# Gate products of the long sequence: half of them by pairs with seven half products, and moved ahead of the units

## The chip, the core and the metric

The kernel runs on one NeuronCore of a Trainium2 chip. The metric is device time of one launch in microseconds (us); the kernel before takes 2138.08 us in the median of three runs (2135.49 to 2138.51).

The core has five instruction queues. TensorE (PE) multiplies matrices out of the on-chip memory SBUF into accumulator banks (PSUM). VectorE (DVE), ScalarE (ACT) and GpSimd (POOL) do the elementwise work. SyncE (SP) issues most of the DMAs. Each queue runs in order, and semaphores tie the queues together.

## The reference, cut to what matters

One layer runs over a short sequence (`x_prompt`, 512 tokens) and a long one (`x_sample`, 1024 tokens), model width 1024:

```
u = x * (1 + scale) + shift                        # T x 1024
proj = u @ w_in                                    # nine segments, for the units A (HGRN2) and R (retention)
y_a, y_r = unit A(proj), unit R(proj)              # T x 1024 each
g_a, g_r = split(sigmoid(u @ w_mg + b_mg))         # w_mg is 1024 x 2048: the gates
s = (g_a * (y_a @ w_pa) + g_r * (y_r @ w_pb)) @ w_out
out = layer_norm(ALPHA * x + (1 + gate) * s) * ln_g + ln_b
```

The change concerns `u @ w_mg` of the long sequence.

## The kernel before, in words

Every large product has float32 accuracy: each operand is split into a high and a low part (type F32R), and three of the four part products are added, low activation times high weight, high times low, high times high. So one output piece of 128 columns by 512 tokens, with 1024 rows to sum over in k = 0 to 7, is 24 matmuls of 512 columns in one PSUM bank (`gemm_f`, L305). There are three such banks (`gbank`), used in turn; a bank is free again when ACT or DVE has read it.

The class `Stream` (L26) holds the weights in the order of use. A raw piece of 512 KB is loaded by SP into one of two buffers. `tick()` has ACT copy it to the high part (L94), `flush()` has DVE (in one stretch POOL) subtract to get the low part (L103). Four split pieces can stand ready.

The sequence g = 0 is the short one, g = 1 the long one, as two blocks b of 512 tokens. Each goes through units (8 A and 4 R for g = 1), then `gates(g)` (L814), then for each block `pblock` (products with `w_pa` and `w_pb`) and `oblock` (product with `w_out`, then layer norm). The order is written out by hand: `interleave` emits the steps of a large product (the filler) and between them stages of elementwise work, spread by weight, and the ticks of the weights. Within an engine, work runs in the order in which it was emitted.

`gates(1)` stands behind the last unit: two blocks of 16 pieces, each piece loaded and split for each block. After 512 columns ACT takes the sigmoid (L826) and issues the store to DRAM (`gd`, L827). In the last block the loads of `pblock`'s first operand `y` begin at the fifth piece (`load_y`, L843).

The layer norm of the last `oblock` of g = 0 ends in four `finish` stages (L911 to L930). In each, DVE makes mean and variance (L914), POOL makes the inverse root (L915, L916), DVE and ACT scale two halves (L919, L925, L928), POOL adds to one half (L929), and SP stores both (L930). They are handed over in `more` and are interleaved with `pre(us[0])`, the 144 matmuls that open the units of g = 1.

Of the kernel before, what the change touches and what calls it, by code (L numbers as in the profile page):

```python
# [17 lines left out]
ALPHA = 2.0 ** 0.25  # L18
LEVELS = (1, 2, 4, 8, 16, 32, 64)
# [6 lines left out]
class Stream:  # L26
    """The weights in order of use: raw pieces are loaded, split into two F32R parts, used, released."""

    def __init__(self, nc, raw_pool, w_pool, ring, raw_bufs, load):
        self.nc, self.raw_pool, self.w_pool = nc, raw_pool, w_pool  # L30
        self.ring, self.raw_bufs, self.load = ring, raw_bufs, load
        self.todo = []
        self.n_load = self.n_split = self.n_got = 0
        self.used = 0
        self.raws = {}
        self.tiles = {}
        self.parts = []
        self.lo = nc.vector
        self.rest = None

# [15 lines left out]
    def open(self, j):  # L56
        """the slots of a piece, if they are free"""
        kind, ps = self.todo[j]
        need = 2 if kind == "t" else 1
        if self.used + need > self.ring:  # L60
            return False
        self.used += need
        if kind == "t":
            h = self.w_pool.tile([128, NK, 256], F32R, name="wh", tag="w", bufs=self.ring)
            l = self.w_pool.tile([128, NK, 256], F32R, name="wl", tag="w", bufs=self.ring)
            self.tiles[j] = (h, l)
            self.parts = [(h[:, :, 128 * i:128 * i + 128], l[:, :, 128 * i:128 * i + 128]) for i in range(2)]
        else:
            shape = [128, 2, 768] if kind == "k" else [128, 2, NK, 128]
            w = self.w_pool.tile(shape, F32R, name="w", tag="w", bufs=self.ring)  # L70
            self.tiles[j] = (w[:, 0], w[:, 1])
            self.parts = [self.tiles[j]]
        return True

    def tick(self):
        """split the next raw piece, if there is room; its low part follows with flush()"""
        self.flush()
        self.pump_loads()
        j = self.n_split
# [9 lines left out]
        i = len(ps) - len(self.parts)  # L89
        hi, lo = self.parts.pop(0)  # L90
        raw = self.raws[j, i]
        if kind == "k":
            raw = raw.rearrange("p k n -> p (k n)")[:, 0:768]
        self.nc.scalar.activation(out=hi, in_=raw, func=AF.Copy)  # L94
        self.rest = (hi, lo, raw, j, i)
        return True

    def flush(self):
# [5 lines left out]
        del self.raws[j, i]  # L104
# [58 lines left out]
def layer(ctx, tc, x_p, x_s, c_p, c_s, w_ada, b_ada, w_in, hgrn_lb, a_norm_w, ret_decay, w_pa, w_pb, w_mg, b_mg,  # L163
# [5 lines left out]
    at = ctx.enter_context(tc.tile_pool(name="at", bufs=2))  # L169
    wp = ctx.enter_context(tc.tile_pool(name="wp", bufs=4))  # L170
    rp = ctx.enter_context(tc.tile_pool(name="rp", bufs=2))
    up = ctx.enter_context(tc.tile_pool(name="up", bufs=4))
    dp = ctx.enter_context(tc.tile_pool(name="scr", bufs=1, space=bass.MemoryType.DRAM))
# [4 lines left out]
    BUFS = {"X": 4, "T1": 2, "T2": 2, "T4": 2, "T8": 2, "T16": 2, "T32": 2, "T64": 2, "T128": 2, "KM": 2, "q": 2,  # L178
            "D": 2, "A": 2, "V": 3, "G": 3, "sg": 2, "Kt": 2, "S": 2, "y": 2, "yT": 2}

    def sb(tag, shape, dt=F32, name=None):
        return at.tile(shape, dt, name=name or tag, tag=tag, bufs=BUFS[tag])

# [30 lines left out]
    gd = [dp.tile([16, 128, NT[g]], F32, name=f"gd{g}") for g in range(2)]  # L214
    xs, outs = (x_p, x_s), (out_p, out_s)

# [32 lines left out]

    def order_pre(u):  # L250
        if u.kind == "A":
            for ls in u.wl:
                h = u.lanes[ls[0]][0]
                for seg in range(3):
                    ws.add("f", (w_in, 1024 * seg + 128 * h))
# [23 lines left out]
    for g in range(2):  # L279
# [4 lines left out]
        else:  # L284
            order_pre(us[0])
# [4 lines left out]
        for b in range(NT[g] // 512):  # L290
            for n in range(16):
# [13 lines left out]
    def gemm_f(ps, w, a):  # L305
        """ps[n, t] += sum_k w[k, n] a[k, t]; a: (hi, lo) as lists of [128, 512] over k"""
# [9 lines left out]
    def gemm_t(ps, w, a, t0, k0=0, k1=NK):  # L316
        """ps[t, n] += sum_k a[k, t] w[k, n]"""
# [49 lines left out]
    def pre_A(u):  # L367
        g = u.g
        prep_A(u)
        for ls in u.wl:  # L370
            for seg in range(3):
# [5 lines left out]
                ws.done(j)  # L377

# [27 lines left out]
    def update(u, l, h):  # L406
        """decays of blocks of h become those of blocks of 2h"""
# [406 lines left out]
    def gates(g):  # L814
        for b in range(NT[g] // 512):
            for n in range(16):
                j, w = ws.get()
                if b == NT[g] // 512 - 1:
                    if n == 4:
                        more_y = load_y(g, 0, 0)  # L820
                    if n >= 4 and more_y:
                        more_y.pop(0)()
                ps = gbank([128, 512])
                yield from gemm_f(ps, w, u_f(g, b))
                t = sb("sg", [128, 512])
                S.activation(out=t, in_=ps, func=AF.Sigmoid, bias=vec[:, 48 + n:49 + n])  # L826
                S.dma_start(gd[g][n, :, 512 * b:512 * b + 512], t)  # L827
# [78 lines left out]
    def oblock(g, b, st, last):  # L906
# [49 lines left out]
        # the last rows of s come last  # L956
# [62 lines left out]
    def u_parts():  # L1019
        """the next part of each product of u_stage that still lacks one"""  # L1020
# [6 lines left out]
    def ada_mm(ps, w):  # L1027
        """silu(c) times columns of w_ada: four sums over k, rows 32 j and 32 j + 1 of ps"""
# [4 lines left out]
    def ada_out(ps, row, jobs):  # L1033
        """the sum of the four, with the columns on the partitions, plus a bias and a constant"""
# [6 lines left out]
    def startup():  # L1041
# [47 lines left out]
        # silu(c) = c / (1 + exp(-c))  # L1089
# [12 lines left out]
        def bounds():  # L1102
# [3 lines left out]
            # softmax over the one layer, its cumulative sum less its first row  # L1106
# [11 lines left out]
        def log_sigmoids():  # L1118
            # lg = log_sigmoid(r) = min(r, 0) - log1p(e), e = exp(-|r|); log1p(e) = 2 atanh(z), z = e / (2 + e)
# [118 lines left out]
    PRE = {"A": 31.1, "R": 20.9}  # L1238
    MID = {"A": 20.9, "R": 41.9}

    def run(gen):
        for _ in gen:
            pass

    with tc.manual_schedule():
        startup()
        more = []
        for g in range(2):
            us = groups[g]
            if g:  # L1250
                interleave(pre(us[0]), 12.0, more, marks, ws)
            for i, u in enumerate(us):
                st = stages_A(u) if u.kind == "A" else stages_R(u)
                if i + 1 < len(us):
                    nx = us[i + 1]
                    interleave(chain(mid(u), pre(nx)), MID[u.kind] + PRE[nx.kind], st, marks, ws, LEAD_IN)
                else:
                    interleave(chain(mid(u), gates(g)), MID[u.kind] + 60.0, st, marks, ws)
            more = []
            nb = NT[g] // 512  # L1260
            for b in range(nb):
# [13 lines left out]
                more = st["finish"]  # L1275

# [51 lines left out]
```

## Time and profile before

| quantity | value |
|---|---|
| median of three runs | 2138.08 us (2135.49 to 2138.51) |
| profiled execution, span from first to last instruction | 2135.2 us |
| PE busy | 2108.5 us, 99% |
| DVE, ACT, POOL busy | 1122.3 us, 746.7 us, 437.7 us |
| share of the last chain that is PE | 95% |
| median of the runs less the span of the profile | 2.9 us |

The page gives no separate time for the profiled execution beyond its span; the lowest of the three runs lies 0.3 us above that span, the median 2.9 us.

How to read it: PE is busy for nearly the whole span, so a matmul that goes saves its own step, and a new wait of PE costs its own length. The elementwise engines are busy half the time or less, but what counts is whether they finish before PE asks for their result.

### The profile page before, as it was taken

Reading aid. Unit: us, or ns where it says so; the run is one execution under the profiler, and the core shown is the slowest. Engines: PE = TensorE matmul, PEld = TensorE weight load, DVE = VectorE, ACT = ScalarE, POOL = GpSimd, SP = SyncE. Lnnn points to the kernel's source line nnn. Section 1 sums busy time; section 2 is a strip of 40 time slices with the busy share of each in tenths; the row PEclk is TensorE's granted clock in tenths of the full one; section 3 lists DMA queues with packets and bytes.
Section 4 is the critical chain, followed back from the end, with each engine's and each line's share of the span. In section 5 each row is a group of like instructions: output and inputs, shape, how many; then the busy total and the mean of one; then the engine's idle time right before and its main releaser. Section 6 shows DMA issues by size and latency. Waiting matters only on the chain.

```text
span 2135.2 us, 45792 instructions
## 1 busy us (share of the span) xinstructions
PE 2108.5 (99%) x19331; PEld 1892.8 (89%) x19331; DVE 1122.3 (53%) x2242; ACT 746.7 (35%) x1570; POOL 437.7 (20%) x668
## 2 busy tenths in 40 slices
PE   7999999999999999999999999999999999999997
PEld 5898899998888988899889889999999888889887
DVE  4856764644334965554565457353543442245657
ACT  3644553223322534444444435212121233322221
POOL 3322233321000332121121214332322100000101
PEclk9999999999999999999999999999999999999999
DMA  9322323246776421111111211212212256577752
GB/s 285 111 84 85 92 85 106 70 129 187 226 243 201 140 80 61 41 50 61 41 61 41 70 31 61 65 41 65 85 40 85 84 163 211 185 234 225 242 184 80
DMA packets 340205, 247.29 MB, mean 116 GB/s; under 512 B 9564, under 2 KB 303680, under 8 KB 338976
## 3 DMA queue, kind: packets, MB, share of 16 engines
q1 hardware_dynamic: 332112, 229.75, 34.9%
q10 hardware_dynamic: 6944, 12.59, 1.5%
q8 instruction: 152, 2.49, 0.5%
q0 software_dynamic: 944, 2.02, 0.3%
q14 instruction: 53, 0.43, 0.1%
HBM read 199.23 MB, written 45.10 MB: 114 GB/s over the span
## 4 chain that ended last, share of the span: by engine, by line
PE 95%; DMA 1%; DVE 1%; POOL 1%; issue 1%; ACT 1%; SPq 0%; POOLq 0%; DVEq 0%; ACTq 0%
PE g L310 41%; PE g L321 38%; PE l L542 2%; PE l L430 2%; PE t L505 2%; PE l L459 1%; PE l L742 1%; PE l L740 1%; PE t L677 1%; PE g L1171 1%; PE t L489 1%; PE l L1171 1%; PE t L707 1%; PE l L725 1%; PE t L1031 1%
## 5 line engine op out<-in xcount | busy, mean ns | idle before, releaser
L321 PE MATMUL g<-wh,u 128*128 128x256 f32 x3840 | 736.2, 287 | 0.0
L310 PE MATMUL g<-u,w 128*128 128x512 f32 x2736 | 671.7, 397 | 0.0
L321 PEld LDWEIGHTS g<-wh,u 128*128 128x128 f32 x3840 | 609.5, 191 | 8.9 <-issue 4.0
L310 PEld LDWEIGHTS g<-u,w 128*128 128x128 f32 x2736 | 499.7, 188 | 100.7 <-issue 1.2
L321 PE MATMUL g<-wl,u 128*128 128x256 f32 x1920 | 542.6, 283 | 0.0
L321 PEld LDWEIGHTS g<-wl,u 128*128 128x128 f32 x1920 | 367.1, 191 | 0.1
L103 DVE TENSOR_TENSOR w<-raw,w 128x1024 fp32r<-128x1024 f32 (+1 forms) x144 | 174.8, 1215 | 209.6 <-ACT w L94 209.5
L310 PE MATMUL g<-y,w 128*128 128x512 f32 x1152 | 261.8, 389 | 0.0
L310 PEld LDWEIGHTS g<-y,w 128*128 128x128 f32 x1152 | 216.1, 188 | 44.9
L414 DVE TENSOR_TENSOR X<-X,T 128x512 f32<-128x512 f32 x336 | 219.1, 698 | 22.2 <-issue 20.4
L94 ACT ACTIVATE w<-raw 128x1024 fp32r<-128x1024 f32 (+1 forms) x146 | 151.5, 1047 | 138.9 <-DMA raw<-in_w_pb 36.4
L103 DVE TENSOR_TENSOR wl<-raw,wh 128x1024 fp32r<-128x1024 f32 x98 | 122.6, 1262 | 104.2 <-ACT wh L94 104.2
L416 POOL TENSOR_TENSOR T<-T 128x512 f32<-128x512 f32 (+6 forms) x168 | 119.7, 739 | 83.6 <-DVE T L343 81.6
L94 ACT ACTIVATE wh<-raw 128x1024 fp32r<-128x1024 f32 x104 | 106.8, 1055 | 38.2 <-PE g L321 33.7
L321 PE MATMUL g<-wh,sl 128*128 128x256 f32 x384 | 109.0, 284 | 0.0
L446 POOL COPY A<-D 32x128 f32<-32x128 f32 x96 | 57.4, 598 | 248.4 <-DVE D L439 245.4
L321 PE MATMUL g<-wl,sh 128*128 128x256 f32 x384 | 107.6, 280 | 0.0
L321 PE MATMUL g<-wh,sh 128*128 128x256 f32 x384 | 107.6, 280 | 0.0
L403 ACT ACTIVATE KM<-X 128x256 f32<-128x256 f32 x120 | 51.5, 430 | 126.2 <-DVE X L414 122.5
L915 POOL TENSOR_SCALAR stat<-stat 128x1 f32<-128x1 f32 x12 | 9.2, 765 | 373.7 <-DVE stat L914 373.7
L826 ACT ACTIVATE sg<-g,vec 128x512 f32<-128x512 f32 x48 | 33.0, 687 | 127.2 <-PE g L310 127.2
L321 PEld LDWEIGHTS g<-wl,sh 128*128 128x128 f32 x384 | 73.3, 191 | 0.1
(197 smaller groups left out, 2390.7 us busy)
## 6 DMA issues: line engine op xcount, KB each, us to landing
raw<-in_w_in SPq DMA_DIRECT2D x122, 512.0 KB, 4.1
yd<-yT SPq DMA_DIRECT2D x96, 256.0 KB, 2.1
raw<-in_w_mg SPq DMA_DIRECT2D x48, 512.0 KB, 3.9
y<-yd SPq DMA_DIRECT2D x24, 1024.0 KB, 8.9
gd<-sg ACTq DMA_DIRECT2D x48, 256.0 KB, 2.7
raw<-in_w_pa SPq DMA_DIRECT2D x24, 512.0 KB, 4.7
raw<-in_w_pb SPq DMA_DIRECT2D x24, 512.0 KB, 4.0
gt<-gd SPq DMA_DIRECT2D x48, 256.0 KB, 4.7
```

What stands on the lines that cost most here:

```text
L94: self.nc.scalar.activation(out=hi, in_=raw, func=AF.Copy)
L103: self.lo.tensor_tensor(out=lo, in0=raw, in1=hi.bitcast(F32), op=ALU.subtract)
L310: T.matmul(ps, w[wi][:, k, :], a[ai](k), start=n == 0, stop=n == 3 * NK - 1)
L321: T.matmul(ps, a[ai](k, t0), w[wi][:, k, :], start=k == 0 and n == 0, stop=k == NK - 1 and ai == wi)
L403: S.activation(out=K4[:, :, 0, :], in_=halves(u.X[l][:, 0, :], h)[:, :, 0, :], func=AF.Copy)
L414: V.tensor_tensor(out=v, in0=v, in1=f, op=ALU.mult)
L416: G.tensor_tensor(out=T2, in0=Tv[:, :, :, 0], in1=Tv[:, :, :, 1], op=ALU.mult)
L430: T.matmul(ps[32 * i:32 * i + 32, c, :], km[:, c0:c0 + 32], qq, start=True, stop=True, tile_position=(0, 32 * i))
L446: G.tensor_copy(out=A[32 * i:32 * i + 32, :, 32 * i:32 * i + 32], in_=u.Dt[l][32 * i:32 * i + 32, :, :])
L505: T.matmul(ps[:, m, :], kt[:, m, :], u.Vt[l][:, c, :], start=True, stop=True)
L542: T.matmul(ps[:, c, :], a, b, start=i == 0, stop=i == len(mm) - 1)
L1171: T.matmul(acc[l, seg], w[wi][:, n0:n0 + 128], uh[0, 0, ai][:, k, :], start=k == 0 and n == 0, stop=k == 7 and n == 2)
```

## The change

For g = 1 the sixteen gate pieces are cut in three, and twelve of them go in front of the units:

- Pieces 0 to 3 (`FIRST`) are made first, for both blocks from one split of each weight piece. In between, twelve stages of `build_comb` make four combinations S1 to S4 of the activations. With a11, a12 for block 0 (first and second half of the 1024 rows) and a21, a22 for block 1, these are S1 = a21 + a22, S2 = S1 - a11, S3 = a11 - a21, S4 = a12 - S2, each split into a high and a low part, in four rounds k = 0 to 3.
- Pieces 4 to 11 are made as four pairs (`gemm_pair`). A pair is two weight pieces, combined on POOL (`combine`), times two token blocks, with seven half products of 12 matmuls (84) in place of 96 matmuls; DVE adds the partial results.
- Pieces 12 to 15 (`LAST`) stay behind the last unit, in the old form, 8 products of 24 matmuls. The loads of `y` begin at the first of the last four.
- The four `finish` stages of g = 0 are emitted one after the other ahead of `FIRST` (`run_stages`), no longer between steps of a product.
- The pool of the units' tiles is closed and opened three times, since `FIRST` and the pairs need its space. `EARLY` is empty, so `fetch`, `qd` and `fd` do nothing.

The diff, cut to what acts:

```diff
@@ class Stream
+        if kind in COMBINED:
+            m = COMBINED.index(kind)
+            if m == 0:
+                self.pairs[j] = self.combine(self.raws[j, 0], self.raws[j, 1])
+            raw = self.pairs[j - m][m]
+            if m == 2:
+                hi, lo = hi[:, 0:4], lo[:, 0:4]
@@ order of the weights, g = 1
+            for n in FIRST:
+                ws.add("f", (w_mg, 128 * n))
+            for seg, x in PAIRED:
+                order_pair(*((w_mg, 128 * x) if seg is None else (w_in, 1024 * seg + 128 * x)))
             order_pre(us[0])
...
-            for n in range(16):
+            for n in LAST if g else range(16):
                 ws.add("f", (w_mg, 128 * n))
@@ gates
+    def build_comb():
...
+            def sums():
+                for x, (b, half) in enumerate(((1, 0), (1, 1), (0, 0), (0, 1))):
+                    t = f[b, half] = sb("e", [128, 512], name="f")
+                    hi, lo = [uh[1, b, p][:, 4 * half + k, :].bitcast(F32) for p in range(2)]
+                    (V, G)[x % 2].tensor_tensor(out=t, in0=hi, in1=lo, op=ALU.add)
+            def mixes():
+                a21, a22, a11, a12 = f[1, 0], f[1, 1], f[0, 0], f[0, 1]
+                V.tensor_tensor(out=a22, in0=a21, in1=a22, op=ALU.add)
+                G.tensor_tensor(out=a21, in0=a11, in1=a21, op=ALU.subtract)
+                V.tensor_tensor(out=a11, in0=a22, in1=a11, op=ALU.subtract)
+                V.tensor_tensor(out=a12, in0=a12, in1=a11, op=ALU.subtract)
+            def parts():
+                for i, t in enumerate((f[1, 1], f[0, 0], f[1, 0], f[0, 1])):
+                    S.activation(out=comb[i][0][:, k, :], in_=t, func=AF.Copy)
+                    (V, G)[i % 2].tensor_tensor(out=comb[i][1][:, k, :], in0=t,
+                                                in1=comb[i][0][:, k, :].bitcast(F32), op=ALU.subtract)
+            return [Stage(sums), Stage(mixes), Stage(parts)]
+        return [s_ for k in range(4) for s_ in piece(k)]
+    def combine(r0, r1):
...
+        G.tensor_tensor(out=t12[:, 0:4], in0=b12, in1=b11, op=ALU.subtract)
+        G.tensor_tensor(out=t12[:, 4:8], in0=b22, in1=t12[:, 0:4], op=ALU.subtract)
+        G.tensor_tensor(out=t34[:, 0:4], in0=b22, in1=b12, op=ALU.subtract)
+        G.tensor_tensor(out=t34[:, 4:8], in0=b21, in1=t12[:, 4:8], op=ALU.subtract)
+    def gemm_pair(done):
...
+        yield from half(p1, w0, 0, a11, True, False)
+        yield from half(p6, w1, 4, s2, True, True)
+        S.activation(out=u2, in_=p1, func=AF.Copy)
+        yield from half(p1, w0, 4, a12, False, True)
+        V.tensor_tensor(out=u2, in0=p6, in1=u2, op=ALU.add)
+        done(0, 0, p1)
+        yield from half(p5, w1, 0, s1, True, False)
+        V.tensor_tensor(out=u4, in0=p5, in1=u2, op=ALU.add)
+        yield from half(p7, w3, 0, s3, True, False)
+        V.tensor_tensor(out=u4, in0=p7, in1=u4, op=ALU.add)
+        yield from half(p5, w2, 0, s4, False, True)
+        V.tensor_tensor(out=c12, in0=p5, in1=u2, op=ALU.add)
+        done(1, 1, u4)
+        yield from half(p7, w3, 4, a22, False, True)
+        V.tensor_tensor(out=u2, in0=p7, in1=u2, op=ALU.add)
@@ main loop, g = 1
-                interleave(pre(us[0]), 12.0, more, marks, ws)
+                close_pool()
+                open_pool("st")
+                interleave(gates(1, FIRST, True), 41.9, build_comb(), marks, ws)
+                interleave(pair_products(), 1.0, [], marks, ws)
+                close_pool()
+                open_pool("at1")
+                run(pre(us[0]))
...
                 more = st["finish"]
+                if g == 0:
+                    run_stages(more)
```

How the order moves on PE, at the end of the last `oblock` of g = 0 (names: sh, sl the parts of its operand, wh, wl, w weights, u the activations, c the combinations). First the kernel before, then the changed one:

```order
L321 MATMUL g<-wh,sl 128x256
L321 MATMUL g<-wl,sh 128x256
L321 MATMUL g<-wh,sh 128x256
L310 MATMUL g<-u,w 128x512 x144
L321 MATMUL g<-wh,u 128x256
```

```order
L369 MATMUL g<-wh,sl 128x256
L369 MATMUL g<-wl,sh 128x256
L369 MATMUL g<-wh,sh 128x256
L358 MATMUL g<-u,w 128x512 x192
L939 MATMUL g<-u,w 128x512 x12
L939 MATMUL g<-c,w 128x512 x12
L939 MATMUL g<-u,w 128x512 x12
L939 MATMUL g<-c,w 128x512 x36
L939 MATMUL g<-u,w 128x512 x24
```

The 144 matmuls of `pre(us[0])` now come behind 192 of `FIRST` and four times 84 of the pairs; the second half product of a pair (c, twelve matmuls) reads S2.

On ACT at the same place, before and then changed (h the rows of the layer norm, sg a sigmoid, f and c the sums and combinations, gd the stored gates):

```order
L928 ACTIVATE h<-h,stat 128x512
L353 ACTIVATE sg<-g 128x512
L928 ACTIVATE h<-h,stat 128x512 x2
L353 ACTIVATE sg<-g 128x512
L94 ACTIVATE wh<-raw 128x8x128
L928 ACTIVATE h<-h,stat 128x512
```

```order
L1114 ACTIVATE h<-h,stat 128x512 x4
L104 ACTIVATE w<-raw 128x1024 x2
L885 ACTIVATE sg<-g,vec 128x512
L886 DMA gd_103<-sg 128x512
L885 ACTIVATE sg<-g,vec 128x512
L886 DMA gd_103<-sg 128x512
L104 ACTIVATE w<-raw 128x1024
L914 ACTIVATE c<-f 128x512 x4
```

The first bank of the new products (sg) is read behind all four scalings of `finish` and two splits, where before a bank was read behind one scaling.

On POOL, the changed kernel behind the four `finish` (t is the pair's combined weight):

```order
L1115 TENSOR_TENSOR h<-h,lb 128x512
L903 TENSOR_TENSOR f<-u 128x512 x2
L908 TENSOR_TENSOR f<-f 128x512
L926 TENSOR_TENSOR t_8552<-raw 128x512
L927 TENSOR_TENSOR t_8552<-raw,t_8552 128x512
L928 TENSOR_TENSOR t_8553<-raw 128x512
L929 TENSOR_TENSOR t_8553<-raw,t_8552 128x512
L915 TENSOR_TENSOR c<-f,c 128x512 x2
```

Before, the next row there was L416 of the first unit. Of each round POOL has five operations on 128x512, and the four of the first pair's weights stand inside the first round.

## Rows read from the trace of the kernel before

**Rows 1.** The page, busy time and share of the span.

```profile
PE 2108.5 (99%) x19331; PEld 1892.8 (89%) x19331; DVE 1122.3 (53%) x2242; ACT 746.7 (35%) x1570; POOL 437.7 (20%) x668
```

**Rows 2.** The chain that ended last: start us, us, what.

```profile
598.18 87.08 PE g L310 x384
738.50 32.66 PE g L310 x144
```

**Rows 3.** Timeline of DVE at the seam: start, us, line, out<-in.

```profile
739.22 0.68 DVE L1015 TENSOR_TENSOR u<-y,u 128x512 fp32r<-128x512 f32 x1
739.82 0.68 DVE L937 TENSOR_TENSOR sg<-g,gt 128x512 f32<-128x512 f32 x1
...
742.72 1.22 DVE L103 TENSOR_TENSOR w<-raw,w 128x1024 fp32r<-128x1024 f32 x1
743.86 0.26 DVE L914 BATCH_NORM_AGGREGATE stat<-stat 128x2 f32<-128x24 f32 x1
744.15 1.41 DVE L919 SCALAR_TENSOR_TENSOR h<-h,stat,lg 128x512 f32<-128x512 f32 x2
```

**Rows 4.** Timeline of POOL at the seam, the first `finish` and its successor.

```profile
744.20 0.79 POOL L915 TENSOR_SCALAR stat<-stat 128x1 f32<-128x1 f32 x1 [11.50 <-DVE stat L914]
745.07 0.92 POOL L916 TENSOR_TENSOR stat<-stat,nhalf 128x1 f32<-128x1 f32 x1
746.83 1.29 POOL L929 TENSOR_TENSOR h<-h,lb 128x512 f32<-128x512 f32 x1 [0.84 <-ACT h L928]
748.28 0.79 POOL L915 TENSOR_SCALAR stat<-stat 128x1 f32<-128x1 f32 x1 [0.15 <-DVE stat L914]
```

**Rows 5.** Timeline of ACT at the seam: a scaling and a split.

```profile
746.03 0.73 ACT L928 ACTIVATE h<-h,stat 128x512 f32<-128x512 f32 x1 [5.11 <-POOL stat L916]
...
754.98 1.05 ACT L94 ACTIVATE wh<-raw 128x1024 fp32r<-128x1024 f32 x1
```

**Rows 6.** Timeline of ACT in the gates of g = 1.

```profile
1799.32 0.69 ACT L826 ACTIVATE sg<-g,vec 128x512 f32<-128x512 f32 x1 [3.24 <-PE g L310]
```

**Rows 7.** DMA issues, 740 to 790 us: KB each, median us to landing.

```profile
out<-h SPq DMA_DIRECT2D x8, 256.0 KB, 2.0
```

**Rows 8.** Timelines of POOL and DVE where both meet.

```profile
750.91 1.29 POOL L929 TENSOR_TENSOR h<-h,lb 128x512 f32<-128x512 f32 x1 [0.83 <-ACT h L928]
...
751.08 2.34 DVE L919 SCALAR_TENSOR_TENSOR h<-h,stat,lg 128x512 f32<-128x512 f32 x2
```

**Rows 9.** Groups of POOL by shape: count, busy us, mean ns.

```profile
L929 POOL TENSOR_TENSOR h<-h,lb 128x512 f32<-128x512 f32 x11 | 14.2, 1292 | 9.2 <-ACT h L928 9.2
```

**Rows 10.** Timeline of POOL, a product of the same size beside an idle DVE.

```profile
136.28 1.04 POOL L416 TENSOR_TENSOR T<-T 128x512 f32<-128x512 f32 x1
```

**Rows 11.** Stretches at the end: us, PE, PEld, DVE, ACT, POOL busy, PEclk, DMA.

```profile
2122.00:2124.00 2.00, 1.68 (x15) 1.48 (x13) 1.93 (x4) 0.00 (x0) 1.27 (x2) 1.00 0.00 0
2124.00:2126.00 2.00, 0.00 (x0) 0.00 (x0) 1.51 (x4) 0.72 (x1) 1.17 (x2) 1.00 0.00 0
2126.00:2128.00 2.00, 0.00 (x0) 0.00 (x0) 1.93 (x4) 0.00 (x0) 0.53 (x1) 0.50 0.65 252
```

**Rows 12.** Timeline of PE in the startup.

```profile
16.30 1.94 PE L1031 MATMUL t<-wa,cw 128*32 128x256 f32 x16 [3.18 <-DMA wa<-in_w_ada]
...
18.93 1.43 PE L1171 MATMUL g<-u,w 128*128 128x512 f32 x3
20.20 0.50 PE L1036 MATMUL t<-pair,row 128*128 128x2 f32 x4
20.56 1.63 PE L1171 MATMUL g<-u,w 128*128 128x512 f32 x6
```

**Rows 13.** The loads of y (L848), all 24 in the kernel.

```profile
DMA to landing us min/median/max: 5.8/8.9/12.2
```

More of the change, by code (lines that the diff above doesn't have):

```diff
@@ L39, in __init__ @@
         self.rest = None
+        self.pairs = {}
     def add(self, kind, *pieces):
@@ L248, in layer, with order_pair @@
     ]
+    EARLY = ()
+    FIRST, LAST = range(4), range(12, 16)
+    PAIRED = [(None, n) for n in range(4, 12, 2)] + [(seg, h) for seg in EARLY for h in range(0, 8, 2)]
+    def order_pair(src, c0):
+        ws.add("s0", (src, c0), (src, c0 + 128))
+        for kind in COMBINED[1:]:
+            ws.add(kind)
     def order_pre(u):
@@ L254, in order_pre @@
                 for seg in range(3):
-                    ws.add("f", (w_in, 1024 * seg + 128 * h))
+                    if u.g == 0 or seg not in EARLY:
+                        ws.add("f", (w_in, 1024 * seg + 128 * h))
         else:
@@ L369, in pre_A @@
         prep_A(u)
+        if g:
+            fetch(u)
         for ls in u.wl:
-            for seg in range(3):
+            for seg in [seg for seg in range(3) if g == 0 or seg not in EARLY]:
                 j, w = ws.get()
@@ L377, in pre_A, with fetch @@
                 ws.done(j)
+    def fetch(u):
+        for l in range(2):
+            h, b = u.lanes[l]
+            if 0 in EARLY:
+                u.X[l] = sb("X", [128, 4, 512])
+                u.q[l] = sb("q", [128, 512])
+                nc.sync.dma_start(u.q[l], qd[h, b])
+            for seg in (1, 2):
+                if seg in EARLY:
+                    ip, im = ((2, 0), (1, 3))[seg - 1]
+                    nc.sync.dma_start(u.X[l][:, ip, :], fd[seg - 1, h, b])
+        for l in range(2):
+            for seg in (1, 2):
+                if seg in EARLY:
+                    ip, im = ((2, 0), (1, 3))[seg - 1]
+                    X = u.X[l]
+                    S.activation(out=X[:, im, :], in_=X[:, ip, :], func=AF.Sigmoid, scale=-1.0)
+                    S.activation(out=X[:, ip, :], in_=X[:, ip, :], func=AF.Sigmoid)
     def mid_A(u):
@@ new lines, in pair_products, with done @@
+    def pair_products():
+        for seg, x in PAIRED:
+            def done(b, i, what):
+                t = what if i + b else sb("e", [128, 512], name="c11")
+                if seg is None:
+                    gate_evac(1, x + i, b, what, t)
+                elif seg == 0:
+                    sg = sb("sg", [128, 512])
+                    S.activation(out=sg, in_=what, func=AF.Sigmoid)
+                    V.scalar_tensor_tensor(out=t, in0=what, scalar=qsc[:, x + i:x + i + 1], in1=sg, op0=ALU.mult,
+                                           op1=ALU.mult)
+                    S.dma_start(qd[x + i, b], t)
+                else:
+                    if i + b == 0:
+                        S.activation(out=t, in_=what, func=AF.Copy)
+                    S.dma_start(fd[seg - 1, x + i, b], t)
+            yield from gemm_pair(done)
@@ L817, in gates @@
+    def gates(g, ns=range(16), both=False):
+        nb = NT[g] // 512
+        for bs in [range(nb)] if both else [(b,) for b in range(nb)]:
+            for n in ns:
                 j, w = ws.get()
-                if b == NT[g] // 512 - 1:
-                    if n == 4:
+                if not both and bs[0] == nb - 1:
+                    if n == ns[4 if g == 0 else 0]:
                         more_y = load_y(g, 0, 0)
-                    if n >= 4 and more_y:
+                    if n >= ns[4 if g == 0 else 0] and more_y:
@@ L822, in gates @@
                         more_y.pop(0)()
[L823 to L827, printed above, removed]
+                for b in bs:
+                    ps = gbank([128, 512])
+                    yield from gemm_f(ps, w, u_f(g, b))
+                    gate_evac(g, n, b, ps, sb("e" if both else "sg", [128, 512], name="sg"))
@@ L1237, in layer, with run_stages @@
     LEAD_IN = 2.5
-    PRE = {"A": 31.1, "R": 20.9}
+    PRE = {("A", 0): 31.1, ("R", 0): 20.9, ("A", 1): 31.1 * (3 - len(EARLY)) / 3, ("R", 1): 20.9}
     MID = {"A": 20.9, "R": 41.9}
     def run(gen):
-        for _ in gen:
-            pass
+        interleave(gen, 1.0, [], marks, ws)
+    def run_stages(stages):
+        while stages:
+            stages.pop(0).fn()
     with tc.manual_schedule():
```

82 lines of the change are left out of this document (71 added, 11 removed).

## The prediction, made before the changed kernel was run

> **What bounds the kernel now.** I read the page's busy times first: PE works for 99% of the span [rows 1], so the reader is to see that elementwise work is hidden today. Then the chain that ended last, for the step of a matmul and for the moment at which the changed part begins: 384 matmuls of 512 columns took 87.08 us, 0.2268 us each, and the 144 matmuls of `pre(us[0])` began at 738.50 us without a pause [rows 2]. I call this moment T. Then the timelines of DVE, POOL and ACT around T, since the change puts a lot of their work right behind it [rows 3 to 5]. The reader is to see three things there: how long one `finish` holds POOL, in which order ACT reads banks, and what DVE and POOL do to each other.
>
> **What goes.** A pair has 84 matmuls where before 96 stood; four pairs save 48 matmuls, 48 x 0.2268 = 10.9 us of PE. The other gate products keep their number. Splits of weights become fewer (20 raw pieces in place of 32), but these lay beside PE, so I count nothing for them.
>
> **The first wait, at the fourth product of `FIRST`.** In the changed order DVE reaches the first `finish` where a split stood, at 742.7 us [rows 3]. POOL starts 0.34 us after DVE's mean (743.86 to 744.20), so at 743.1, and one `finish` after the other costs it 4.08 us (744.20 to 748.28), because POOL itself waits for ACT in the middle [rows 3, 4]. ACT's scaling begins 1.83 us into each cycle and takes 0.73 [rows 4, 5]. So the fourth ends at 743.1 + 3 x 4.08 + 1.83 + 0.73 = 757.9. Behind it on ACT stand two splits of 1.05 and only then the first sigmoid, 0.69 [rows 5, 6]: the first bank is free at about 760.7. There are three banks of 24 matmuls (5.44 us) each, so PE wants it at T + 16.3 = 754.8 and waits 5.9 us. Before, the four `finish` were spread between products and PE did not wait.
>
> **The second wait, which contains the first: S2 is late.** PE needs the last low part of S2 after 192 matmuls of `FIRST`, 12 of the first half product and 9 of the second: T + 213 x 0.2268 = 786.8 us. When is it there?
>
> The tiles of the sums lie where the layer norm's rows lay, so the sums wait for the last stores. POOL's fourth addition ends at 743.1 + 3 x 4.08 + 3.92 = 759.3 and the store lands 2.0 us after its issue [rows 4, 7]: 761.3.
>
> From there to that last low part I count in the order. DVE has 25 operations of 128x512 at 0.60 us start to start (739.22 to 739.82), three splits at 1.14 and a half one at 0.60: 19.0 us [rows 3]. POOL has 23 operations of 128x512 (19 of the four rounds, 4 of the first pair's weights); the like one takes 1.29 us [rows 9].
>
> Do the two run side by side? The trace says no. The two scalings L919 take 1.41 us, but 2.34 when they start 0.17 us after POOL's addition began [rows 3, 8]: DVE stood for 0.93 us, until 1.10 us after POOL's start, and POOL's operation is 1.29 long. All operations of the rounds have two inputs in SBUF, as these have. So I count POOL with 1.05 us each during which DVE stands: 24.2 us. Together 43.2 us of turns. Each of the four rounds also has a handing over in which neither holds anything (the difference, then ACT's copy, then the low part); I estimate 0.9 us a round from a scaling of 0.73 on ACT and the 0.1 to 0.2 us that pass between engines in [rows 4], 3.6 us. So S2 is complete at 761.3 + 43.2 + 3.6 = 808.1 us, and PE has waited 21.3 us by then, in pieces: 5.9 at the fourth product, some at the later ones (ACT's sigmoids stand behind its copies of the combinations, which wait for DVE and POOL), the rest inside the first pair.
>
> Bounds. If DVE and POOL do not disturb each other, POOL alone sets the end: 23 x 1.29 = 29.7 us plus about 2.0 us in each round in which it waits for DVE and ACT, less what the pair's weights cover, 6.7: 797.7, 10.9 us late. If POOL keeps DVE out for its full 1.29 us: 29.7 + 19.0 + 3.6 makes 813.6, 26.8 us late. I take 21.3, since [rows 8] are the nearest to what happens here.
>
> The Trainium skill, page "SBUF — State Buffer", section "SBUF: two separate sides", says that a VectorE operation with two SBUF inputs and a GpSimd operation that reads SBUF exclude each other for the whole instruction. By this rule the sum has 26.8 in place of 21.3. The trace agrees that they exclude each other, but DVE came free 0.19 us ahead of POOL's end [rows 8]; the rule's full length is rival C.
>
> **The clock after a wait.** After PE's last matmul the granted clock is 1.00 in 2124 to 2126 us and 0.50 (1.2 of 2.4 GHz) from 2126 on [rows 11]: a stop of a few us brings the lower level. The price of coming back is in the startup: PE works without a pause from 16.30 us, three matmuls of 512 columns from 18.93 still take 1.43 us, six from 20.56 take 1.63 [rows 12]. So at most about 4 us run at half speed, some 2 us lost. I count 1.9 once, for the last stop; what the earlier stops lose is made good by the waits that follow them. Bounds: 0 (no stop long enough) to 3.8 (two count).
>
> **The pairs.** Between a half product and the one that needs its bank again lie 12 matmuls, 2.72 us. In this time DVE has at most a split (1.22) and an addition (0.68, as L937) to do [rows 3]: 1.9, it fits. If POOL's combining stands ahead of the split it is 2.95, 0.2 us too late, perhaps three times in four pairs. I count 0; bounds 0 to 3.
>
> **The end.** The last load of `y` is now issued with the last of the four pieces, 5.44 us before `pblock`, and its part is needed 12 matmuls into it: 8.2 us after issue. Such loads land after 5.8, 8.9 or 12.2 us (least, median, most) [rows 13]. I count 8.9 - 8.2 = 0.7 us, bounds 0 and 4.0. The last unit's stages have less filler beside them (83.8 us in place of 101.9 by the code's own counts), still more than the other R units have (62.8), beside which PE is busy [rows 1]: nothing. New tiles in the reopened pool wait for stores of some 2 us, with three banks of cover: nothing; without the cover, that much once.
>
> **The sum.** -10.9 + 21.3 + 1.9 + 0.7 = +13.0 us. The profiled span is 2135.2; that gives 2148.2, and with the 2.9 us by which the median of the runs stands above it, 2151.
>
> **Rivals.**
> A. DVE and POOL overlap. Then S2 is 10.9 us late, and -10.9 + 10.9 + 1.9 + 0.7 gives +2.6: 2140.7, no change that can be told. Against it stand [rows 8].
> B. Faster, on the other side: they overlap and POOL's operation costs what a product of this size costs beside an idle DVE, 1.04 us [rows 10]. Then the rounds end at 761.3 + 23.9 + 6.7 = 791.9, 5.1 us late, so that the first wait (5.9) is all that remains, and without a clock's fall -10.9 + 5.9 + 0.7 = -4.3: 2133.8. It decides for faster from the point where the whole wait is under 6 us. For it: the sums may behave like the products. Against it: the additions, which are the like operation, took 1.29 us in the mean of eleven [rows 9].
> C. The full exclusion above, 26.8 us late: -10.9 + 26.8 + 1.9 + 0.7 = +18.5, 2156.6.
> D. The upper bounds come together (two clock falls, late additions in the pairs, late `y`): C plus 8, about 2165.
>
> That the change does not do what it says I exclude: the order shows 84 matmuls a pair.
>
> **How the numbers follow.** Two runs can be told apart from about 0.2%, 4.3 us. The forecast (2143 to 2156 as its own range) has 0.58, C 0.17, D 0.05, A 0.13, B 0.07. Slower by over 0.2% (above 2142.4) is forecast, C and D, with a little of A: 0.81. Within 0.2% is most of A: 0.12. Faster is B: 0.07. The range from 2138 to 2161 leaves out B, a little of A and D, under 0.2.
>
> **What would show each step.** In the changed profile: about 48 fewer matmuls of 512 columns with a step still near 0.227 us; PE idle 4 to 8 us before the fourth product of `FIRST`, ended by ACT's sigmoid; PE idle in the second half product of the first pair, ended by a POOL low part; DVE operations of the rounds at 1.5 us and more where POOL runs; a granted clock of 0.50 behind the longest stop; no idle time of PE inside the later pairs; under 4 us at the start of `pblock`. It is wrong if PE's whole idle time in `FIRST` and the first pair is under 11 us, or if DVE keeps its 0.60 us beside POOL.

## The result and the profile after

The changed kernel takes 2151.56 us (median of 4 runs, 2151.25 to 2153.33) against 2137.3 for the kernel before in the same series: a ratio of 1.0070, interval 1.0055 to 1.0084. It is slower by 14.3 us. The span of the profiled execution went from 2135.2 to 2150.0 us, by 14.8.

PE has 48 matmuls fewer and yet as much busy time as in [rows 1]; DVE and POOL work more:

```profile
PE 2108.6 (98%) x19283; PEld 1891.7 (88%) x19283; DVE 1165.2 (54%) x2286; ACT 752.6 (35%) x1586; POOL 493.6 (23%) x704
```

The timeline of PE from the end of the short sequence's last out product, in the place where [rows 2] had 144 matmuls without a pause (start, us, line, shapes, count; in brackets the idle time before and what ended it):

```profile
738.43 16.51 PE L358 MATMUL g<-u,w 128*128 128x512 f32 x72
759.54 23.64 PE L358 MATMUL g<-u,w 128*128 128x512 f32 x96 [4.60 <-ACT sg L885]
785.18 5.73 PE L358 MATMUL g<-u,w 128*128 128x512 f32 x24 [2.00 <-ACT sg L885]
790.75 2.88 PE L939 MATMUL g<-u,w 128*128 128x512 f32 x12
796.60 3.77 PE L939 MATMUL g<-c,w 128*128 128x512 f32 x9 [2.97 <-ACT sg L885]
807.41 1.65 PE L939 MATMUL g<-c,w 128*128 128x512 f32 x3 [7.04 <-POOL c L915]
808.85 3.81 PE L939 MATMUL g<-u,w 128*128 128x512 f32 x12
812.50 8.33 PE L939 MATMUL g<-c,w 128*128 128x512 f32 x36
...
826.11 2.88 PE L939 MATMUL g<-c,w 128*128 128x512 f32 x12
...
845.15 2.88 PE L939 MATMUL g<-c,w 128*128 128x512 f32 x12
```

The reader is to see two things. All stops lie in the four plain pieces and the first pair: 4.60 + 2.00 + 2.97 + 7.04 = 16.6 us. And from there each pair takes 19.04 us (826.11 to 845.15), which is 84 matmuls at 0.2267: no stop in the pairs.

Two groups of rows answer to [rows 8]. DVE first, two of the four `finish` and the first sums:

```profile
743.10 1.42 DVE L1105 SCALAR_TENSOR_TENSOR h<-h,stat,lg 128x512 f32<-128x512 f32 x2
...
745.94 2.34 DVE L1105 SCALAR_TENSOR_TENSOR h<-h,stat,lg 128x512 f32<-128x512 f32 x2
...
759.37 3.44 DVE L903 TENSOR_TENSOR f<-u 128x512 f32<-128x512 f32 x2
```

And POOL: the last addition of `finish`, its first sums, the first combining of weights, the second round's sums, and the last low parts, S2's and then S4's:

```profile
757.10 1.27 POOL L1115 TENSOR_TENSOR h<-h,lb 128x512 f32<-128x512 f32 x1 [0.83 <-ACT h L1114]
758.32 3.94 POOL L903 TENSOR_TENSOR f<-u 128x512 f32<-128x512 f32 x2
...
767.80 1.33 POOL L926 TENSOR_TENSOR t<-raw 128x512 f32<-128x512 f32 x1 [1.88 <-DMA raw<-in_w_mg]
...
777.66 2.54 POOL L903 TENSOR_TENSOR f<-u 128x512 f32<-128x512 f32 x2
...
805.64 3.40 POOL L915 TENSOR_TENSOR c<-f,c 128x512 fp32r<-128x512 f32 x2 [1.47 <-ACT c L914]
```

Two operations of DVE take 1.42 us while POOL has only its 128x1 operations of `finish`, 2.34 beside one addition of POOL and 3.44 beside two sums. POOL's two sums take 3.94 us here and 2.54 in the second round, where DVE waits for the first of them. Both engines hold each other up.

### The profile page after: what moved, and what is told of

Same layout as the page of the kernel before. It is cut to its first block, busy times and chain, and to the rows that moved or that the text cites. A ratio compares the mean times of both kernels' runs of the same rounds, so it can differ in the third digit from the quotient of the medians.

```text
span 2150.0 us, 45795 instructions
## 1 busy us (share of the span) xinstructions
PE 2108.6 (98%) x19283; PEld 1891.7 (88%) x19283; DVE 1165.2 (54%) x2286; ACT 752.6 (35%) x1586; POOL 493.6 (23%) x704
## 4 chain that ended last, share of the span: by engine, by line
PE 61%; DVE 2%; POOL 1%; issue 0%; DMA 0%; ACT 0%; POOLq 0%; DVEq 0%
PE g L369 25%; PE g L358 23%; PE g L939 3%; PE l L612 2%; PE l L500 2%; PE t L575 1%; PE t L747 1%; PE l L812 1%; PE l L810 1%; PE l L529 1%; PE t L559 1%; PE t L777 0%; PE l L795 0%; PE t L636 0%; PE t L843 0%
## 5 line engine op out<-in xcount | busy, mean ns | idle before, releaser
L358 PE MATMUL g<-u,w 128*128 128x512 f32 x2352 | 586.8, 399 | 6.6 <-ACT sg L885 6.6
L358 PEld LDWEIGHTS g<-u,w 128*128 128x128 f32 x2352 | 428.9, 189 | 93.7 <-ACT sg L885 7.4
L113 DVE TENSOR_TENSOR w<-raw,w 128x1024 fp32r<-128x1024 f32 (+2 forms) x132 | 160.6, 1218 | 142.7 <-ACT w L104 142.5
L104 ACT ACTIVATE w<-raw 128x1024 fp32r<-128x1024 f32 (+2 forms) x134 | 137.0, 1033 | 135.0 <-PE g L358 27.7
L369 PEld LDWEIGHTS g<-wh,sl 128*128 128x128 f32 x384 | 73.6, 192 | 0.1
L369 PEld LDWEIGHTS g<-wh,sh 128*128 128x128 f32 x384 | 73.6, 192 | 0.0
```

What stands on the lines that cost most here:

```text
L113: self.lo.tensor_tensor(out=lo, in0=raw, in1=hi.bitcast(F32), op=ALU.subtract)
L358: T.matmul(ps, w[wi][:, k, :], a[ai](k), start=n == 0, stop=n == 3 * NK - 1)
L369: T.matmul(ps, a[ai](k, t0), w[wi][:, k, :], start=k == 0 and n == 0, stop=k == NK - 1 and ai == wi)
```

## The experiments

The kernel before was measured beside each group of runs, with medians from 2135.53 to 2137.3 us; each ratio goes by the one of its own group. Where two groups are compared by their times, some 1 to 2 us of the difference can be the group's.

**The move alone.** All twelve pieces ahead of the units as plain products, nothing built:

```diff
-    FIRST, LAST = range(4), range(12, 16)
+    FIRST, LAST = range(12), range(12, 16)
-    PAIRED = [(None, n) for n in range(4, 12, 2)] + ...
+    PAIRED = [(None, n) for n in ()] + ...
-                interleave(gates(1, FIRST, True), 41.9, build_comb(), marks, ws)
+                interleave(gates(1, FIRST, True), 41.9, [], marks, ws)
```

> The gates ahead of the units, but no pairs: all twelve pieces ahead as plain products, nothing built, the same number of matmuls as before. My theory (S2 late because of its building, the rest small): what is left is the first stop behind the four finish scalings (4.6 us in the changed kernel), about 1.7 us for the one fall of the clock behind it, 0.5 us for the last y load: 2142 to 2146 us, against 2137.3 before. Rival 1 (the move alone explains most of the 14.3 us): 2149 or more. Rival 2 (the move costs nothing): 2137.

Measured: 2146.43 us, ratio 1.0050 (1.0037 to 1.0062). The move by itself costs 10.2 us, 0.4 us above the expected range and short of the first rival's 2149. PE's one wait of over 0.5 us after the startup (waited for: us in total, times, longest):

```profile
PE g L358 <- ACT sg L885: 4.6, 1, 4.6
```

The one stop is the one behind the four `finish` on ACT. The rest of the 9.0 us by which the span grew has no wait. The expected 1.7 us for the clock's return leave 2.7; a slower pace of matmuls, which the expectation did not have, is taken up under "64 bytes".

**No building.** The pairs and the weights' combinations as changed; pieces of u stand in place of S1 to S4, so these eight gate pieces are not computed, and `build_comb()` is left out as in the run above:

```diff
-        s1, s2, s3, s4 = [comb[i] for i in range(4)]
+        s1, s2, s3, s4 = [[uh[1, b, p][:, 4 * x:4 * x + 4, :] for p in range(2)]
+                          for b, x in ((1, 0), (1, 1), (0, 0), (1, 0))]
...
-                interleave(gates(1, FIRST, True), 41.9, build_comb(), marks, ws)
+                interleave(gates(1, FIRST, True), 41.9, [], marks, ws)
```

> The pairs as they are, with 48 matmuls fewer, but the four token combinations are not built: pieces of u stand in their place, so the gates of the eight pieces are not computed (the weights' combinations are still made). Theory: PE never waits for S2, the first stop of 4.6 us and one fall of the clock (1.7 us) stay: 2137.3 - 10.9 + 4.6 + 1.7 + 0.5 = 2133 us, up to 2136. Rival (the half products, the weights' combinations or the pairs' evacuation cost what the 48 matmuls save): 2140 or more.

Measured: 2134.87 us, ratio 0.9995 (0.9986 to 1.0004), as the theory had it. Against the move alone the 48 matmuls give 11.6 us (10.9 in the sum). Against the changed kernel the building of the token combinations costs 16.7, or 15.6 if each is taken against the kernel before of its own group. After the stop of 4.60 us PE goes through to the units:

```profile
758.60 29.99 PE L358 MATMUL g<-u,w 128*128 128x512 f32 x120 [4.60 <-ACT sg L885]
788.43 76.32 PE L939 MATMUL g<-u,w 128*128 128x512 f32 x336
```

**The building on VectorE alone.** In `build_comb`, `G` and `(V, G)[...]` become `V`:

```diff
-                    (V, G)[x % 2].tensor_tensor(out=t, in0=hi, in1=lo, op=ALU.add)
+                    V.tensor_tensor(out=t, in0=hi, in1=lo, op=ALU.add)
```

> All sums, mixes and low parts of the token combinations on VectorE, none on GpSimd. Theory (the two engines hold each other up: each VectorE op beside a GpSimd one takes 0.9 us more): a round is 12 x 0.62 = 7.5 us in place of 11.2, S2 is ready at about 759.4 + 30 + 3.6 for the weights' splits + 3 beside the weights' combinations = 796 instead of 807.4, needed at 786.7: 9 us late instead of 21: 2140 us, range 2137 to 2145. Rival (the round is bound by its hand-overs between engines and by its own operations, without mutual holding): VectorE's 7 ops a round become 12, S2 is not ready sooner: 2151 or more.

Measured: 2142.86 us, ratio 1.0031 (1.0018 to 1.0043): 8.7 us faster than the shared building (7.6 by the groups' own kernels before), though DVE has 12 operations a round in place of 7. The sums and the low parts of the first two rounds on DVE; POOL combines weights from 767.4 to 774.8 us:

```profile
759.77 2.48 DVE L903 TENSOR_TENSOR f<-u 128x512 f32<-128x512 f32 x4
...
771.83 4.67 DVE L903 TENSOR_TENSOR f<-u 128x512 f32<-128x512 f32 x4
...
779.20 2.49 DVE L915 TENSOR_TENSOR c<-f,c 128x512 fp32r<-128x512 f32 x4
```

Four operations take 2.48 us alone and 4.67 beside POOL. PE waits for S2 only from 794.5 to 799.5 us (5.0, where the changed kernel has 2.97 and 7.04). The mutual holding is shown by these rows. How the 8.7 us divide is not: with one engine the waits of DVE for POOL's difference go too, 1.4 us in each round of the changed kernel. VectorE alone is still too slow for 41.9 us of cover: S2 comes 12.4 us after the moment at which a PE without stops would want it (799.5 against 738.83 + 213 x 0.2268 = 787.1).

**The first stop alone.** The four `finish` scalings and additions go from ScalarE and GpSimd to VectorE:

```diff
-                    if q == 0 or (last and i == 3):
+                    if q == 0 or g == 0 or (last and i == 3):
```

> The four finish scalings and additions of the short sequence's second half taken from ScalarE and GpSimd to VectorE, so that ScalarE's first sigmoid of the gates does not stand behind them; all else as changed. Theory (the first stop lies inside S2's lateness): the stop of 4.6 us goes, PE then waits as much longer at S2; only GpSimd's and VectorE's earlier start of the first sums counts, 1 to 2 us: about 2150 us. Rival (stops add up): 2151.6 - 4.6 - 1.7 = 2145 us.

Measured: 2148.49 us, ratio 1.0060 (1.0047 to 1.0073), 3.1 us off the changed kernel (2.0 by the groups' own kernels before); the rival wanted 6.3. The waits of PE after the startup, the three largest:

```profile
PE g L939 <- POOL c L915: 8.5, 1, 8.5
PE g L358 <- ACT sg L885: 6.6, 3, 2.4
PE g L939 <- ACT sg L885: 1.2, 1, 1.2
```

The stop of 4.6 us is gone, and the sum of the stops is 16.3 in place of 16.6: they moved to S2 and to smaller ones. From the first gate product to the fourth half product of the first pair PE needs 73.87 us (737.15 to 811.02), where the changed kernel needs 74.07 (738.43 to 812.50). So of the 1.8 us between the two profiled spans (2150.0 and 2148.2) only 0.2 lies where the edit acts, and 1.3 is an earlier start, ahead of it. On DVE all four L1105 pairs of scalings, now with no addition of POOL beside them, take 1.41 or 1.42 us, which only the first took in the changed kernel; the third:

```profile
748.84 1.41 DVE L1105 SCALAR_TENSOR_TENSOR h<-h,stat,lg 128x512 f32<-128x512 f32 x2
```

**More cover.** Three pairs, six plain pieces ahead of them:

```diff
-    FIRST, LAST = range(4), range(12, 16)
+    FIRST, LAST = range(6), range(12, 16)
-    PAIRED = [(None, n) for n in range(4, 12, 2)] + ...
+    PAIRED = [(None, n) for n in range(6, 12, 2)] + ...
-                interleave(gates(1, FIRST, True), 41.9, build_comb(), marks, ws)
+                interleave(gates(1, FIRST, True), 62.9, build_comb(), marks, ws)
```

> Three pairs instead of four, and six plain pieces ahead of them instead of four; the combinations are built as in the changed kernel, over 62.9 us of products instead of 41.9. Theory (what costs is that S2 is late): 36 matmuls fewer than before give -8.2 us; S2 is needed 21.8 us later, so only the first stop of 4.6 us, one fall of the clock (1.7) and the 3.3 us left open stay: 2137.3 - 8.2 + 4.6 + 1.7 + 3.3 = 2139 us. Rival (the building costs wherever it lies, by holding up splits and gates): 2146 or more.

Measured: 2138.32 us, ratio 1.0007 (0.9998 to 1.0016), the theory's number. The same building, still shared by DVE and POOL, stops PE nowhere; the waits after the startup that exceed 0.5 us are two:

```profile
PE g L358 <- ACT sg L885: 4.6, 1, 4.6
PE g L358 <- DMA y<-yd: 1.2, 1, 1.2
```

So the building as such costs nothing that can be told: without it, three pairs would come to 2134.87 + 2.7 = 2137.6. Placed too close ahead of its use it costs the 13.2 us between this kernel and the changed one, and the 2.7 us that the fourth pair gave there.

**S2 first.** The four pairs kept; all building on VectorE, S1 and S2 of all k ahead of S3, and S4 last:

```diff
-        return [s_ for k in range(4) for s_ in piece(k)]
+        return [Stage(fn(k), w=w) for fn, w in ((first, 2.0), (third, 0.25), (fourth, 0.75)) for k in range(4)]
```

where `first` makes S1 and S2 with their low parts and S3 without, `third` S3's low part, `fourth` S4. The sums that live through several rounds, and the pairs' partial results u2 and u4, get a set of eight buffers of their own for it.

> The same combinations, all on VectorE, in another order: first S1 and S2 of all four k with S3's sums (8 VectorE ops a k, 19.8 us), then S3's low parts, then S4 (3 ops a k). Theory (only S2's lateness costs): S2's last low part at about 759.8 + 19.8 + 5 for the weights' splits = 785, needed at 786.7 + 4.6 + 1.7 for the first stop = 793, S3 and S4 in time: no stop at the pairs, 2135 us as without any building (2134.9). Rival (the building also slows the pairs' own steps, or S4 comes late in place of S2): 2140 or more.

Measured: 2149.22 us, ratio 1.0057 (1.0044 to 1.0069): the theory failed here, and the rival held. PE no longer waits for S2, as expected, but beside the expected stop of 4.60 us it has two others:

```profile
758.69 12.74 PE L358 MATMUL g<-u,w 128*128 128x512 f32 x48 [4.60 <-ACT sg L885]
776.11 18.01 PE L358 MATMUL g<-u,w 128*128 128x512 f32 x72 [4.67 <-ACT sg L885]
...
805.18 5.18 PE L952 MATMUL g<-u,w 128*128 128x512 f32 x12 [5.62 <-ACT u L969]
```

What ACT did ahead of the second and third stop, and DVE's sums of the second and the third k:

```profile
773.40 0.63 ACT L902 ACTIVATE c<-f 128x512 fp32r<-128x512 f32 x1 [7.09 <-DVE f L913]
774.85 0.63 ACT L902 ACTIVATE c<-f 128x512 fp32r<-128x512 f32 x1 [0.82 <-DVE f L915]
775.39 0.67 ACT L885 ACTIVATE sg<-g,vec 128x512 f32<-128x512 f32 x1
...
803.07 0.63 ACT L902 ACTIVATE c<-f 128x512 fp32r<-128x512 f32 x1 [1.51 <-DVE f L928]
...
804.55 0.58 ACT L969 ACTIVATE u<-g 128x512 f32<-128x512 f32 x1
```

```profile
767.62 5.15 DVE L912 TENSOR_TENSOR f<-u 128x512 f32<-128x512 f32 x3
...
776.12 1.89 DVE L912 TENSOR_TENSOR f<-u 128x512 f32<-128x512 f32 x3
```

The copy of a combination stands in ACT's queue and waits 7.09 us for DVE; the sigmoid that frees PE's bank stands behind it. Of these, 3.26 us are again the mutual holding: POOL combines weights from 765.3 to 772.2 us, and DVE's three sums beside it take 5.15 us in place of 1.89. At the pair, the copy of the first half product (L969) stands behind the copy of S4's last part and one split of weights. The building does not only have to be ready: an operation of it in ACT's queue hands its own wait on to the gates behind it.

**S2 first, finish on VectorE.** Both edits.

> As the kernel with S2 first, and the finish scalings and additions on VectorE as well. Theory (now that nothing else is late, the first stop counts in full): 2135 - 4.6 - 1.7 = 2129 us, up to 2133 if ScalarE's sigmoids come behind copies that wait for VectorE (three such stops of 1.9 to 2.4 us came with the finish on VectorE before). Rival (VectorE takes up what ScalarE and GpSimd lose, so that S2 is late again): 2135 or more.

Measured: 2146.98 us, ratio 1.0048 (1.0036 to 1.0061); stops of 7.6 us behind sigmoids (two) and 5.4 behind the copy L969, none at S2. The theory had allowed for sigmoids behind copies that wait for VectorE, but with 4 us (up to 2133); the copy L969 it did not have. The rival's number held and its reason did not: S2 was not late.

**64 bytes.** The span grew by 14.8 us. Waits and clock, less the saved matmuls, explain 12.0 of it; part of the rest sits in the pace of matmuls. The chain of waits gives the long sequence's first out product and the product with y behind it. The kernel before (start, us, what):

```profile
1946.16 45.23 PE g L321 x384
1991.39 87.06 PE g L310 x384
```

The changed kernel:

```profile
1959.21 46.07 PE g L369 x384
2005.28 87.07 PE g L358 x384
```

The edit, in the pools of the changed kernel, which open in the order constants, split weights, raw weights, u and y, the rest:

```diff
+    pad = ctx.enter_context(tc.tile_pool(name="pad", bufs=1))
+    pad.tile([128, 16], F32, name="pad")
     rp = ctx.enter_context(tc.tile_pool(name="rp", bufs=2))
```

> The changed kernel with 64 unused bytes a partition between the weights' tiles and all other tiles, nothing else. It is about 1.7 us which no wait explains: each of the long sequence's two out products takes 46.07 and 46.23 us after the change and 45.23 and 45.39 before, the same instructions; the change moved the weights' tiles in SBUF, so that weights (wh, wl) and sums (sh, sl) now begin at the same byte modulo 512 (256), where before they began at 192 and 256. Theory (the pace of the 256-column matmuls depends on that): the out products go back to 45.2 us each; if the 5760 matmuls of 256 columns with u, whose tiles had one offset in both kernels, follow by the same 0.0022 us each, 12.7 us more: between 2137 and 2150 us. Rival (the places do not matter): 2151.6, the out products stay at 46.1.

Measured: 2132.74 us, ratio 0.9981 (0.9972 to 0.9989): 18.8 us less than the changed kernel, for 64 bytes that nothing uses, and below the expected range, which began at 2137. Its chain:

```profile
1941.66 43.54 PE g L371 x384
1985.20 87.89 PE g L360 x384
```

The matmuls of 256 columns go from 0.1200 to 0.1134 us each (46.07 / 384, 43.54 / 384); those of 512 get slower, from 0.2267 to 0.2289. The same in the kernel before, where constants and all other tiles come ahead of the split weights, so that the pad moves only raw, u and y:

> The kernel before, with 64 unused bytes a partition between the tiles of the split weights and those of the raw weights and of u and y; nothing else. Theory (the pad acts on the pace of the matmuls, whatever the gates' order): what it gave the changed kernel, 18.8 us, less the 1.7 us that the out products and about 1.1 us that the units had already in the kernel before: 2136.7 - 16 = 2121 us (2118 to 2125); the changed kernel is then as much slower at equal places (about 12 us) as without the pad. Rival (the pad mends only what the change had spoiled): 2136.

Measured: 2117.92 us, ratio 0.9919 (0.9905 to 0.9932), 0.1 us below the expected range. With the pad in both kernels the change costs 2132.74 - 2117.92 = 14.8 us (13.7 by the groups' own kernels before; 12.9 between the two profiled spans, 2128.9 and 2116.0), against 14.3 without it: what the pad gives does not come from the change. The tiles still do not lie at equal places, since the pools of the two kernels open in different orders. The out products here too take 43.54 us, and none of their operands moved; the explanation by the operands' own places is refuted. Then 128 bytes in place of 64 (`[128, 32]`):

> The kernel before with 128 unused bytes in place of 64 at the same spot: only the tiles of raw, u and y move. With 64 bytes the out products went from 45.23 to 43.54 us though none of their operands moved, so the pace does not hang on the operands' own places. Theory A (what counts is where those tiles begin modulo 128 bytes): with 128 nothing changes, 2136 us, out products 45.2. Theory B (any shift does it, or the place in some larger unit): 2118 us again, or another time.

Measured: 2146.87 us, ratio 1.0050 (1.0033 to 1.0067). Theory A fails, and of B only the open half, "another time", is left: it is 9.6 us slower than no pad. Its chain:

```profile
1953.85 45.22 PE g L323 x384
1999.07 89.22 PE g L312 x384
2088.29 29.97 PE g L323 x264
```

The first out product keeps the pace of the kernel before (0.1178), the last has that of the 64 bytes (29.97 / 264 = 0.1135), and the product with y is the slowest of all (0.2323). With and without a pad the page of the kernel before lists the same 45792 instructions, so the pad changes places and not the work. What sets the pace stays open.

**What was measured to help, in one.** Three pairs, finish on VectorE, 64 bytes.

> Three pairs behind six plain pieces, the finish scalings and additions on VectorE, and the 64 bytes: what was measured to help, in one. Theory (they add up): 2138.3 - 18.8 for the pad - 4.6 - 1.7 for the first stop = 2113 us, up to 2117 if sigmoids behind ScalarE's copies stop PE as they did with the finish on VectorE before; faster than the kernel before with the pad (2121). Rival (without the first stop S2 is late again, or the sigmoids are): 2120 or more.

Measured: 2112.73 us, ratio 0.9889 (0.9874 to 0.9904), the expected number, and faster than both kernels and than the kernel before with the pad (by 5.2 us). From the first gate product on PE has one wait left, of 0.4 us.

**More pairs.** Eight more, for two of the three input pieces of the A heads (`EARLY = (0, 1)`):

> As the last one, with eight pairs more: the first two of the three input pieces of the long sequence's eight A heads are made by pairs too, ahead of the units, and stored to and fetched from HBM. Theory (the combinations are built once, each further pair is a gain of 12 matmuls): 96 matmuls of 0.2268 us fewer: 2113 - 21.8 = 2091 us. Rival (the units' products were the cover of their VectorE work, and PE waits in the units instead): 2113 or more.

Measured: 2142.22 us, ratio 1.0030 (1.0018 to 1.0041), 29.5 us slower than without them: the rival. PE now waits inside the units; the three largest from the first gate product on:

```profile
PE l L502 <- ACT KM L476: 17.0, 30, 1.1
PE t L638 <- ACT y L629: 8.3, 7, 1.2
PE l L614 <- DVE S L586: 7.1, 7, 1.0
```

With the small ones it is 37.8 us against 0.4; less the 22 us of the 96 matmuls that gives 15.4 of the 25.0 us between the two spans. The other 9.6 were not followed further.

## Why the prediction was right

The forecast was 2151, the time 2151.56. The mechanism came as forecast: S2 late by the turns of DVE and POOL, with one lasting loss by the clock. That the time came within 0.6 us is luck in part. The sum was made against the profiled span, +13.0 forecast and +14.8 measured, so it lacks 1.8 us. The 2.9 us added for the distance of the runs from their profile were 1.6 for the changed kernel (2151.56 against 2150.0), which makes up for 1.3 of them. Term by term:

- **What goes: -10.9.** 48 matmuls fewer by the page; -11.6 between the runs without building and with the move alone.
- **The first wait: 5.9, measured 4.6.** The cause is the one named, a sigmoid behind four scalings and two splits: ACT's first sigmoid began at 758.82 us. The wait was shorter, mostly because one `finish` cost POOL 3.8 us (from 747.04 to 750.83), not the 4.08 of [rows 4]. The forecast gave this wait no price beside the second one, which contains it, and that holds in the changed kernel: with it taken away the stops still sum to 16.3 us. It counts where S2 is in time.
- **S2 late: 21.3, measured 20.7** (807.41 against 738.43 + 213 x 0.2268 = 786.7). That it came so near is luck: errors in its parts cancel. The sums did not wait for the last store to land (761.3): POOL's began at 758.32, right behind its addition, 3 us sooner. From there to S2's last low part it took 49.0 us (758.32 to about 807.4), where 46.8 was counted, 43.2 of turns and 3.6 of handing over. In these 49.0 us DVE and POOL stand still together for only 0.6, never for more than 0.08 at a time. So the handing over was sized 3.0 too high and the turns about 5.2 too low. POOL's wait of 1.88 us for the raw weights of the pair, which the sum did not have, is no such time, since DVE works beside it. What makes the turns longer was not taken apart; the 25 operations counted for DVE leave out two that ran ahead of the end of S2's last low part, in time counted as handing over. That DVE and POOL exclude each other is shown by both runs that took POOL's work away.
- **The clock: 1.9 once, measured 1.7 once.** The granted clock fell behind three of the stops:

```profile
760.00:766.00 6.00, 6.00 (x21) 4.80 (x21) 4.59 (x5) 2.22 (x3) 3.56 (x3) 0.75 0.62 201
...
802.00:808.00 6.00, 0.59 (x1) 0.50 (x2) 4.59 (x7) 3.70 (x6) 3.62 (x3) 0.66 0.02 5
808.00:814.00 6.00, 6.00 (x22) 4.83 (x21) 2.72 (x2) 0.93 (x3) 5.92 (x5) 0.77 0.00 0
```

  (stretch; busy us of PE, weight load, DVE, ACT, POOL; granted clock, DMA share, GB/s). What PE lost at the lower level before S2 (96 matmuls in 23.64 us for 21.8, nine in 3.77 for 2.0) went into the waits that followed, as forecast; behind the last stop the lateness grew from 20.7 to 22.4 (812.50 against 738.43 + 228 x 0.2268).
- **The pairs: 0**, and no stop in them.
- **The end: 0.7, measured 0.46**, PE's wait for `y`:

```profile
1896.33 62.45 PEld L358 LDWEIGHTS g<-y,w 128*128 128x128 f32 x276 [0.46 <-DMA y<-yd]
```

- **What the sum did not have.** -10.9 + 20.7 + 1.7 + 0.5 makes 12.0. Of the 2.8 left, the two out products have 1.7 (46.07 and 46.23 for 45.23 and 45.39, with no wait), and about 1.1 lies in the 958 us of the units and was not followed. Every kernel here with the new order of pools and without the pad has the same 46.07. The forecast has no such term, since it read the change as moving work in time only; the change also moved tiles in SBUF. The runs with pads show that places can set this pace; that they did so here is argued, not shown.

Of the rivals, A and B (no mutual holding, 10.9 and 5.1 us late) fall with the rows of DVE above; C wanted 26.8, and D stands on C. The Trainium skill, page "SBUF — State Buffer", section "SBUF: two separate sides", says that a VectorE operation with two SBUF inputs and a GpSimd operation that reads SBUF hold each other off for the whole instruction. The rows support the holding. As to its length, a pair of DVE scalings that starts 0.16 us into an addition of 1.29 takes 0.92 us more (2.34 against 1.42), as in [rows 8], so part of the addition passes beside DVE. In the rounds it is the same: POOL's last two low parts, which alternate with DVE's, take 3.40 us, 1.70 each. Less the 0.62 of a DVE operation (2.48 for four) that leaves about 1.08 for one of POOL, which takes 1.27 where DVE waits (2.54 for two). The forecast took 1.05.

## What to carry to other kernels

A saving of matmuls is worth its own time only where the operands that it needs are ready: count the building's turns on DVE and POOL as one queue, and put as many products ahead of it as it lasts. Look as well at whose queue the building shares: a copy that waits in ACT's queue holds up the sigmoid that frees PE's bank. And when a change reorders pools, compare the pace of untouched matmuls, since their tiles' places can be worth more than the change.

## What was not expected of the hardware

The pace of matmuls with the same instructions takes one of several values a kernel and stretch, and for the out products of the kernel before even with operands at the same places: 0.1134, 0.1178 or 0.1200 us for 256 columns, 0.2267, 0.2289 or 0.2323 for 512, at a granted clock of 1.00. An unused gap of 64 bytes a partition moves the kernel before by -17.6 us, one of 128 bytes by +9.6. It is no wait, and the pace is even over a whole out product. Which tile's place does it, and how, is open.
